# Gate vectors by weighted row sums inside the feed-forward networks, and one PSUM tile for both score maps of a differential head

## The chip, the cores and the metric

The program runs on one core of one Trainium2 chip. The metric is the device time of one execution in microseconds (us). The median of three runs of the kernel before is 1020.04 us (1017.32 to 1021.83).

## The reference, cut to what matters

One inference step of a two-layer backbone over 384 tokens, in three blocks of 128 (block 0 holds context tokens, blocks 1 and 2 latent ones), model width 1024. Each layer is a mixer, its output projection, and a SwiGLU network of width 2816. Layer 0 mixes by retention and windowed attention, layer 1 by differential attention and a Fourier transform. Each layer needs six modulation vectors per condition (there are two conditions: context and latent), one product of 1 x 1024 by 1024 x 6144:

```
mod = silu(cond) @ w_mod[l] + b_mod[l]
sh1, sc1, g1, sh2, sc2, g2 = split(mod, 6)
u = layer_norm(x) * (1 + sc1) + sh1
x = layer_norm(ALPHA * x + g1 * mixer(u), ...)
u = layer_norm(x) * (1 + sc2) + sh2
x = layer_norm(ALPHA * x + g2 * swiglu(u), ...)
```

The vector that the change is about is g2, number 5 of each layer's six, which is needed only once the network's output is complete. The other part is the differential attention, which has two score maps per head, each of 64 channels:

```
s = einsum('bqhmd,bkhmd->bhmqk', q, k) * 64 ** -0.5      # m = 0, 1
p = softmax(s);  p = p[:, :, 0] - lam * p[:, :, 1]
```

## The kernel before, in words

Everything lies in one program; when it is built, a planner fixes the order of instructions on each engine: of those that its own cost estimates show ready, the one of highest priority comes first (the order of the program text, raised by `boost`, L116). On the chip nothing overtakes on its engine. Matrix products with weights are split: a weight tile arrives by DMA (issued by SyncE's queue, SP) into a ring of five raw tiles, ScalarE casts it to a rounded copy (L173), VectorE makes the remainder (L175), and TensorE multiplies three times (rounded by rounded, and the two cross terms, L377, L518, L542). The copies lie in rings of five.

**The modulation vectors** are made in two ways. `mod_pe` (L223) loads a vector's 1024 x 1024 weights in eight raw tiles and multiplies each on TensorE with the conditions as a stationary operand of 32 columns: 32 matmuls of 128x256, four to a k-step. They are plain float32 matmuls, which stand as two records each in the trace, so 64 records for one vector. `mod_steps` (L237) loads the same eight tiles into another ring (`big`, four tiles, shared with the residual sums), and ScalarE (L246, first tile) and VectorE (L249, the seven others, two instructions each, one per condition) add them up with the conditions as per-partition weights into two tiles z; then eight matmuls with ones (16 records, L254) sum over the partitions, and two VectorE instructions (L258 or L260, L261) pick the rows. A gate vector (number 2 or 5) is then written to DRAM in eight small DMAs on SP (`mod_scratch`, L281) and read back broadcast by `load_g` (L414, two DMAs). Its bias comes by four DMAs on ScalarE's queue (L220).

**Where they run.** `WMODS` names the vectors that `w_out_phase` (L434) makes by `mod_pe`: g2 of layer 0 in layer 0's output projection, g2 of layer 1 in layer 1's. The order there is written by hand (`WORDER`, L38): P is the projection of a block with its residual, A and B its two layer norms, F the transposition to `u`, H the head of the network (its first 256 columns, gate `hg` and up `hu`, then the transposes `ht`), M the vector by `mod_pe`. M stands between the heads of blocks 1 and 2 (at the end: `X H1 M H2`). M's matmuls are not boosted and come late in the text, so the planner puts them where it has nothing else ready for TensorE. `SMODS` names the vectors that the network makes by `mod_steps`: five in layer 0, none in layer 1. The network (`ffn_phase`, L494) has ten rounds of two slots, each slot one projection (48 matmuls, L542) and, in the first 15 slots, one step of the down projection (18 matmuls, L518). A vector takes three slots: four weight tiles in each of the first two (`MSTEP`), a pause in the third; its last matmuls come at the next slot (`steps`, L1433). Five vectors take slots 0 to 14 of 20, and the last one's matmuls fall behind slot 15. The five last slots have no down step and are shorter.

**The differential scores** (`mixer_cd`, L1150). `scores` (L1245) works through 18 items (six heads, three blocks), two ahead. For an item, `sc1` (L1206) takes for each map one of four single-bank PSUM tiles, multiplies 64 channels (map 0 from partitions 0 to 63, map 1 from 64 to 127; 128 keys for block 0, else 384), and reduces the maximum over the keys (L1217); then one small instruction (L1219) and two exponentials (L1223). `sc2` (L1228) normalises, subtracts the maps (L1232 to L1234) and transposes (`td`). The items are mixed with the projections `cd` (L377) and the Fourier products (`y`, `z`). The window attention of layer 0 does its pair already as `sc1` does after the change: `win1` (L855) takes a pair of banks (`ws`) and one maximum for both (L872).

Of the kernel before, what the change touches and what calls it, by code (L numbers as in the profile page):

```python
# [14 lines left out]
AF = mybir.ActivationFunctionType  # L15
ALU = mybir.AluOpType
AX = mybir.AxisListType
PSUM = bass.MemoryType.PSUM

P = 128  # L20
# [5 lines left out]
NFP = D_FF // 256  # L26
HOLD = 4
RHOLD = (3, 5)
WMODS = (((0, 5),), ((1, 5),))
TMODS = ()  # L30
SMODS = (((1, 1), (1, 0), (1, 3), (1, 4), (1, 2)), ())
NLNW = 8
AORDER = "Q0 R0 W4 T G0 D V0 M0 Q1 W12 M1 G1 C0 E M2 N1 R1 N2 V1 C1 X N0 N4 N3 N5"
NIDLE = (5, 4)
# [30 lines left out]
def trunk_kernel(ctx: ExitStack, tc: tile.TileContext, a: dict):  # L65
    nc = tc.nc
    mm = nc.tensor.matmul
    V, S, G, SY = nc.vector, nc.scalar, nc.gpsimd, nc.sync
# [4 lines left out]
    def opened(name, **kw):  # L73
        st = ExitStack()
        return st.enter_context(pool(name, **kw)), st
# [6 lines left out]
    def bankA(name):  # L82
        return psA.tile([P, 512], F32, tag="A", name=name)
# [19 lines left out]
    def small(shape, name):  # L103
        tick[0] += 1
        n = 1
        for s in shape[1:]:
            n *= s
        return perm.tile(shape, F32, tag=f"sm{n}", name=f"{name}{tick[0]}", bufs=SMALL[n])
# [4 lines left out]
    def mid(shape, name):  # L113
        return perm.tile(shape, F32, tag="uf", name=name, bufs=3)

    def boost(f, *args, **kw):  # L116
        with tc.high_priority(offset=BOOST):
            return f(*args, **kw)  # L118

    def hmm(*args, **kw):  # L120
        return boost(mm, *args, **kw)
# [1028 lines left out]
    def mixer_cd(u, cat, pto, u1, t1):  # L1150
        o_k = a["o_diff_k"][0, 0].rearrange("t h m d -> t (h m d)")
        o_v = a["o_diff_v"][0, 0].rearrange("t h d -> t (h d)")
        slab = cd_slab
        bk = Banks("pcd", S=4)
        ap, ap_es = opened("attn_cd")
        rope_of[0] = ap.tile([P, 2, 2, 64], F32, name="rope1")
        S.dma_start(rope_of[0], a["k_rope"].rearrange("b p s d -> p b s d"))
        if True:
            nlam, sub = lamd["nlam"], lamd["sub"]
            dqT = ap.tile([P, H_DIFF, NTOK], F32, name="dqT")  # L1160
            dkT = ap.tile([P, H_DIFF, 512], F32, name="dkT")
# [4 lines left out]
            for i, n in ((0, 4), (4, 2)):  # L1166
                t = mid([P, 512], f"ck{i}")
# [38 lines left out]
            def sc1(b, h):  # L1206
                nk = 1 if b == 0 else 3
                k0 = 0 if b == 0 else P
                w = nk * P
                nm = small([P, 2], "dnm")  # L1210
                sums = small([P, 2], "dsum")
                pss = []
                for m in range(2):
                    rows = slice(64 * m, 64 * m + 64)
                    ps = bk("S", f"ds{b}_{h}_{m}")
                    hmm(ps[:, 0:w], dqT[rows, h, b * P : (b + 1) * P], dkT[rows, h, k0 : k0 + w], start=True, stop=True)
                    V.reduce_max(nm[:, m : m + 1], ps[:, 0:w], AX.X)  # L1217
                    pss.append(ps)
                V.tensor_scalar(nm, nm, -0.125, None, ALU.mult)  # L1219
                pm = []  # L1220
                for m in range(2):
                    t = ap.tile([P, 384], F32, tag="p", name=f"dp{b}_{h}_{m}", bufs=5)
                    S.activation(t[:, 0:w], pss[m][:, 0:w], AF.Exp, bias=nm[:, m : m + 1], scale=0.125,  # L1223
                                 accum_out=sums[:, m : m + 1])
                    pm.append(t)
                st_of[b, h] = (pm, sums)
# [18 lines left out]
            def scores(upto):  # L1245
                while state["n2"] < upto:
                    while state["n1"] < min(state["n2"] + 2, len(items)) and (state["n1"] < upto or upto == len(items)):
                        sc1(*items[state["n1"]])
                        state["n1"] += 1
                    sc2(*items[state["n2"]])  # L1250
                    state["n2"] += 1
# [59 lines left out]
            for b in range(NB):  # L1311
                ps = bankA(f"cd4_{b}")
# [6 lines left out]
            for b in range(NB):  # L1319
                ps = bankA(f"cd3_{b}")  # L1320
# [23 lines left out]
    m = {}  # L1344
    xscr = dram.tile([NB, P, D], F32, tag="xscr", name="xscr")
    for l in range(2):
# [9 lines left out]
        if l == 0:  # L1356
            def mod_ab(v, bk):
                mp = mod_pe(0, v, bk("M", f"mod0_{v}"))
                if v == 2:
                    m[0, v] = mod_scratch(mp, f"0_{v}")  # L1360
                else:
                    m[0, v] = mod_cols(mp, 0, v, bk("M", f"modt0_{v}"))

            pre, wxr_es = mixer_ab(u, cat, early, early_es, ap1, ap1_es, pto, *first, [lambda bk, v=v: mod_ab(v, bk) for v in (2, 3, 4)])
        else:
            cat, cat_es = open_cat(1)
            mixer_cd(u, cat, pto, m["s1"], m["t1"])
            pre, wxr_es = [], None
# [11 lines left out]
        hh = tuple(lnp.tile([P, NHEAD, NTOK], F32R, name=f"hh{q}{l}") for q in "rl")  # L1380
        w_out_phase(l, pre, cat, x, gt, lnv, u2, m[l, 3], m[l, 4], wx, hh, bankTO, WMODS[l])
        if wxr_es is not None:
# [37 lines left out]
        def all_mods(todo):  # L1420
            for ll, v in todo:
                out = []
                for pause in mod_steps(ll, v, out):
                    yield pause
                nm = f"{ll}_{v}"
                if v in (2, 5):
                    m[ll, v] = mod_scratch(out[0][0], nm)
                else:
                    m[ll, v] = mod_cols(out[0][0], ll, v, out[0][1])

        gen = all_mods(SMODS[l])

# [90 lines left out]
```

## Time and profile before

| | |
|---|---|
| median of three runs | 1020.04 us |
| profiled execution, its own time | 1018.55 us |
| its span in the trace | 1016.8 us |
| TensorE matmul busy, share of the span | 98% |
| VectorE busy | 63% |
| ScalarE busy | 43% |
| mean granted TensorE clock | 0.997 |

The span runs from the first to the last instruction of the profiled execution; 1.75 us of its own time lie outside. A line of the timeline is: start, duration, engine, line of the kernel, operation, output and inputs by the program's names, shapes, number of instructions merged, and in brackets the idle time before it and what ended that. The step from one row's start to the next row's start is the time that a stream of matmuls really takes; a row's own duration is longer, since matmuls overlap.

### The profile page before, as it was taken

To read this page: it belongs to the slowest core of one execution; us is meant where nothing else is said; L and a number is where in the kernel's file an instruction comes from. 1 tells how busy PE (TensorE), PEld (TensorE's weight loads), DVE (VectorE), ACT (ScalarE), POOL (GpSimd) and SP (SyncE) were. 2 spreads that over 40 slices of the span, in tenths; PEclk is the share of its full clock that TensorE was granted. 3 is DMA by queue.
4 is the path that set the end of the run, shared out by engine and by line. 5 is a ranking of instruction groups with operands and counts; after the bars stand their busy time and mean duration, and the time that the engine had idled before them with its cause. 6 is when DMAs were issued, how large, how long until landed. Compare 5 with 4: busy or idle time off the path is not lost.

```text
span 1016.8 us, 14891 instructions
## 1 busy us (share of the span) xinstructions
PE 996.9 (98%) x5679; PEld 829.7 (82%) x5679; DVE 637.9 (63%) x1356; ACT 432.9 (43%) x786; POOL 1.2 (0%) x5
## 2 busy tenths in 40 slices
PE   9999999999999999999999999999999999999996
PEld 4775567688898988989987766787889999999985
DVE  5477558588785977968567677558843333335554
ACT  3385533227543333333428555544833333333410
POOL 0000000000000000000000000000000000000000
PEclk9999999999999999999999999999999999999998
DMA  9975446472896767676615322235574444444401
GB/s 305 294 203 187 146 132 205 171 254 94 281 301 219 217 211 253 208 235 208 207 63 161 95 88 93 83 103 224 184 252 146 125 125 124 125 125 127 161 22 41
DMA packets 109703, 172.85 MB, mean 170 GB/s; under 512 B 10176, under 2 KB 78272, under 8 KB 109632
## 3 DMA queue, kind: packets, MB, share of 16 engines
q1 hardware_dynamic: 106960, 170.87, 52.8%
q10 hardware_dynamic: 2672, 1.04, 0.4%
q8 instruction: 44, 0.72, 0.3%
q14 instruction: 27, 0.22, 0.1%
HBM read 167.52 MB, written 4.36 MB: 169 GB/s over the span
## 4 chain that ended last, share of the span: by engine, by line
PE 91%; DMA 3%; DVE 3%; ACT 2%; issue 1%; ACTq 0%; DVEq 0%
PE dn L518 17%; PE wu L542 17%; PE wg L542 17%; PE cd L377 8%; PE wo L377 6%; PE rvg L377 3%; PE s L377 3%; PE rqk L377 2%; DMA rawm<-in_w_mod 2%; PE ds L118 2%; PE hg L377 2%; PE mod L118 1%; PE hu L377 1%; PE ms L118 1%; PE po L118 1%; PE wpo L118 1%
## 5 line engine op out<-in xcount | busy, mean ns | idle before, releaser
L542 PE MATMUL wg<-ulf,r_wg 128*128 128x384 f32 x320 | 108.4, 339 | 0.0
L542 PE MATMUL wu<-ulf,r_wu 128*128 128x384 f32 x320 | 108.3, 338 | 0.0
L542 PE MATMUL wu<-urf,r_wu 128*128 128x384 f32 x320 | 108.2, 339 | 0.0
L542 PE MATMUL wg<-urf,l_wg 128*128 128x384 f32 x320 | 108.1, 338 | 0.0
L542 PE MATMUL wu<-urf,l_wu 128*128 128x384 f32 x320 | 108.1, 338 | 0.0
L542 PE MATMUL wg<-urf,r_wg 128*128 128x384 f32 x320 | 108.0, 339 | 0.0
L175 DVE TENSOR_TENSOR l_wg<-raw_wg,r_wg 128x1024 fp32r<-128x1024 f32 x40 | 48.7, 1223 | 68.4 <-ACT r_wg L173 68.4
L249 DVE SCALAR_TENSOR_TENSOR z<-mraw,cs,z 128x1024 f32<-128x1024 f32 x70 | 86.3, 1280 | 8.3 <-DMA mraw<-in_w_mod 8.0
L175 DVE TENSOR_TENSOR l_wd<-raw_wd,r_wd 128x1024 fp32r<-128x1024 f32 x36 | 44.0, 1223 | 53.7 <-ACT r_wd L173 53.7
L173 ACT CAST r_wd<-raw_wd 128x1024 fp32r<-128x1024 f32 x36 | 37.8, 1050 | 87.0 <-PE wu L542 40.1
L175 DVE TENSOR_TENSOR l_wu<-raw_wu,r_wu 128x1024 fp32r<-128x1024 f32 x40 | 48.6, 1222 | 40.1 <-ACT r_wu L173 40.1
L173 ACT CAST r_wg<-raw_wg 128x1024 fp32r<-128x1024 f32 x40 | 42.0, 1050 | 73.0 <-PE dn L518 29.9
L173 ACT CAST r_wu<-raw_wu 128x1024 fp32r<-128x1024 f32 x40 | 42.0, 1049 | 64.6 <-issue 24.2
L518 PE MATMUL dn<-l_wd,hr 128*128 128x512 f32 x168 | 66.6, 396 | 0.0
L518 PE MATMUL dn<-r_wd,hr 128*128 128x512 f32 x168 | 66.5, 396 | 0.0
L518 PE MATMUL dn<-r_wd,hl 128*128 128x512 f32 x168 | 66.5, 396 | 0.0
L542 PEld LDWEIGHTS wg<-urf,r_wg 128*128 128x128 f32 x320 | 60.1, 188 | 1.9 <-issue 0.8
L542 PEld LDWEIGHTS wu<-urf,r_wu 128*128 128x128 f32 x320 | 60.1, 188 | 1.7 <-ACT r_wg L173 0.8
L542 PEld LDWEIGHTS wu<-ulf,r_wu 128*128 128x128 f32 x320 | 60.1, 188 | 0.5
L542 PEld LDWEIGHTS wg<-ulf,r_wg 128*128 128x128 f32 x320 | 60.1, 188 | 0.5
L542 PEld LDWEIGHTS wg<-urf,l_wg 128*128 128x128 f32 x320 | 60.1, 188 | 0.0
L542 PEld LDWEIGHTS wu<-urf,l_wu 128*128 128x128 f32 x320 | 60.1, 188 | 0.0
(418 smaller groups left out, 2180.0 us busy)
## 6 DMA issues: line engine op xcount, KB each, us to landing
raw_wd<-in_w_down SPq DMA_DIRECT2D x44, 512.0 KB
rawm<-in_w_mod SPq DMA_DIRECT2D x40, 512.0 KB
mraw<-in_w_mod SPq DMA_DIRECT2D x40, 512.0 KB
raw_wg<-in_w_gate SPq DMA_DIRECT2D x40, 512.0 KB
raw_wu<-in_w_up SPq DMA_DIRECT2D x40, 512.0 KB
raw_cd<-in_w_in_cd SPq DMA_DIRECT2D x20, 512.0 KB
ms<-in_w_mod SPq DMA_DIRECT2D x16, 512.0 KB
raw_rqk<-in_w_in_ab SPq DMA_DIRECT2D x16, 256.0 KB
```

The costliest lines, as they stand in the source:

```text
L118: return f(*args, **kw)
L173: S.copy(r, t)
L175: V.tensor_tensor(lo, t, r, ALU.subtract)
L249: V.scalar_tensor_tensor(z[c], t, cs[:, c, k : k + 1], z[c], ALU.mult, ALU.add)
L377: op = mm(ps[:, col : col + width], u[pu][:, k0 + kk, b * P : (b + 1) * P], (r, lo)[pw][:, kk, :], start=(first and i == 0 and pu + pw == ...
L518: mm(acc[b, nh], h[fc][ph][:, b * P : (b + 1) * P], wrl[pw][:, nh * 512 : (nh + 1) * 512], start=(fc == 0 and ph + pw == 0), stop=(last an ...
L542: mm(ps[j][:, 0:NTOK], un[i][pw][:, k, j * P : (j + 1) * P], u2[pu][:, 4 * i + k, :], start=(i == 0 and k == 0 and pu + pw == 0), stop=(i ...
```

## The change

Layer 0's g2 becomes the first of six vectors made by `mod_steps` in layer 0's network, layer 1's g2 the only one in layer 1's network; no vector is made in `w_out_phase` any more. In the differential scores the two maps of an item share a tile of two banks (two such tiles instead of four single ones), one instruction takes both maxima, and the exponentials read the halves.

```diff
-WMODS = (((0, 5),), ((1, 5),))
+WMODS = ((), ())
-SMODS = (((1, 1), (1, 0), (1, 3), (1, 4), (1, 2)), ())
+SMODS = (((0, 5), (1, 1), (1, 0), (1, 3), (1, 4), (1, 2)), ((1, 5),))
...
-        bk = Banks("pcd", S=4)
+        bk = Banks("pcd", S=2)
...
-                pss = []
+                ps = bk.pair("S", f"ds{b}_{h}")
                 for m in range(2):
                     rows = slice(64 * m, 64 * m + 64)
-                    ps = bk("S", f"ds{b}_{h}_{m}")
-                    hmm(ps[:, 0:w], dqT[rows, h, b * P : (b + 1) * P], dkT[rows, h, k0 : k0 + w], start=True, stop=True)
-                    V.reduce_max(nm[:, m : m + 1], ps[:, 0:w], AX.X)
-                    pss.append(ps)
+                    hmm(ps[:, m, 0:w], dqT[rows, h, b * P : (b + 1) * P], dkT[rows, h, k0 : k0 + w], start=True, stop=True)
+                V.reduce_max(nm, ps[:, :, 0:w], AX.X)
...
-                    S.activation(t[:, 0:w], pss[m][:, 0:w], AF.Exp, bias=nm[:, m : m + 1], scale=0.125,
+                    S.activation(t[:, 0:w], ps[:, m, 0:w], AF.Exp, bias=nm[:, m : m + 1], scale=0.125,
```

## Rows read from the trace of the kernel before

**Rows 1.** The page: the span, the busy time of three engines with its share and the number of instructions, and the chain that ended last by engine.
```profile
span 1016.8 us, 14891 instructions
PE 996.9 (98%) x5679; PEld 829.7 (82%) x5679; DVE 637.9 (63%) x1356; ACT 432.9 (43%) x786; POOL 1.2 (0%) x5
...
PE 91%; DMA 3%; DVE 3%; ACT 2%; issue 1%; ACTq 0%; DVEq 0%
```
**Rows 2.** Busy time by stretch: the end of layer 0's output phase, layer 0's network to the end of slot 15, its four last slots, the stretch of the scores, what follows them, and the end of layer 1's output phase. Columns: stretch and its length, busy us (instructions) of TensorE matmul, TensorE weight load, VectorE, ScalarE and GpSimd, granted clock, DMA share, GB/s.
```profile
245.40:270.80 25.40, 25.40 (x229) 21.38 (x229) 18.76 (x48) 19.68 (x36) 0.00 (x0) 1.00 0.62 205
270.80:476.20 205.40, 205.40 (x1122) 188.94 (x1120) 161.29 (x166) 72.98 (x89) 0.00 (x0) 1.00 0.74 236
476.20:511.10 34.90, 34.90 (x209) 34.28 (x209) 19.66 (x22) 15.91 (x20) 0.00 (x0) 1.00 0.62 195
574.40:640.30 65.90, 64.86 (x293) 42.55 (x292) 48.91 (x125) 36.40 (x100) 0.00 (x0) 1.00 0.23 72
640.30:673.50 33.20, 33.20 (x154) 26.34 (x152) 13.24 (x21) 16.03 (x36) 0.00 (x0) 1.00 0.26 91
719.70:744.80 25.10, 25.10 (x231) 21.47 (x230) 16.66 (x47) 16.85 (x34) 0.00 (x0) 1.00 0.62 201
```
**Rows 3.** The same view, of the instructions on the tile `mw` alone (the matmuls of `mod_pe` in the two output phases). Columns: stretch and length, busy us (records) of TensorE matmul, weight load and VectorE, granted clock, DMA share, GB/s.
```profile
245.40:270.80 25.40, 5.51 (x64) 1.93 (x64) 0.42 (x1) 1.00 0.62 205
719.70:744.80 25.10, 4.90 (x64) 1.79 (x64) 0.41 (x1) 1.00 0.62 201
```
**Rows 4.** The timeline at the end of layer 0's output phase (`hg`, `hu` head of the network, `urf`, `ulf` its input by the two halves of the channels).
```profile
252.40 1.07 PE L229 MATMUL mw<-rawm,cmod 128*32 128x256 f32 x16
253.77 1.50 PE L229 MATMUL mw<-rawm,cmod 128*32 128x256 f32 x22
254.14 0.62 ACT L332 CAST urf<-ufo 128x512 fp32r<-128x512 f32 x1
255.61 0.37 PE L377 MATMUL hg<-r_gh,urf 128*128 128x256 f32 x1
257.27 1.16 ACT L246 ACTIVATE z<-mraw,cs 128x1024 f32<-128x1024 f32 x1
261.49 0.69 DVE L333 TENSOR_TENSOR ulf<-ufo,urf 128x512 fp32r<-128x512 f32 x1
263.11 1.07 PE L229 MATMUL mw<-rawm,cmod 128*32 128x256 f32 x16
265.04 0.39 PE L377 MATMUL hg<-r_gh,urf 128*128 128x256 f32 x1
```
**Rows 5.** The same place in layer 1.
```profile
728.17 1.50 PE L229 MATMUL mw<-rawm,cmod 128*32 128x256 f32 x24
728.77 0.61 ACT L332 CAST urf<-ufo 128x512 fp32r<-128x512 f32 x1
729.60 0.39 PE L377 MATMUL hg<-r_gh,urf 128*128 128x256 f32 x1
736.33 0.69 DVE L333 TENSOR_TENSOR ulf<-ufo,urf 128x512 fp32r<-128x512 f32 x1
736.58 1.07 PE L229 MATMUL mw<-rawm,cmod 128*32 128x256 f32 x16
738.95 0.39 PE L377 MATMUL hg<-r_gh,urf 128*128 128x256 f32 x1
746.84 0.44 PE L118 MATMUL ht<-ident,hsg 128*128 128x128 f32 x2 [1.22 <-DVE hsg L480]
```
**Rows 6.** The vectors by row sums in layer 0's network: the group of all weighted sums on VectorE (busy us, mean ns of one, idle time before them), and the timeline of the last of the five vectors: the matmuls of the vector before it, its first and last sums, and its own matmuls.
```profile
L249 DVE SCALAR_TENSOR_TENSOR z<-mraw,cs,z 128x1024 f32<-128x1024 f32 x70 | 86.3, 1280 | 8.3 <-DMA mraw<-in_w_mod 8.0
...
440.79 1.07 PE L254 MATMUL mod<-z,ones 128*32 128x256 f32 x16
446.07 4.87 DVE L249 SCALAR_TENSOR_TENSOR z<-mraw,cs,z 128x1024 f32<-128x1024 f32 x4 [1.10 <-DMA mraw<-in_w_mod]
466.00 2.48 DVE L249 SCALAR_TENSOR_TENSOR z<-mraw,cs,z 128x1024 f32<-128x1024 f32 x2 [0.69 <-DMA mraw<-in_w_mod]
476.22 1.07 PE L254 MATMUL mod<-z,ones 128*32 128x256 f32 x16
```
**Rows 7.** The differential scores on TensorE: the tile `ds` in the stretch of the scores (columns as in Rows 2, without GpSimd), and the timeline of five places. An item's two matmuls are four records; the shapes are those of 128 keys and 384 keys.
```profile
574.40:640.30 65.90, 19.75 (x72) 8.10 (x72) 15.29 (x35) 17.95 (x65) 1.00 0.23 72
...
574.49 0.49 PE L118 MATMUL ds<-dkT,dqT 64*128 64x128 f32 x4
582.65 0.92 PE L118 MATMUL ds<-dkT,dqT 64*128 64x384 f32 x4
597.71 0.91 PE L118 MATMUL ds<-dkT,dqT 64*128 64x384 f32 x2
620.77 0.49 PE L118 MATMUL ds<-dkT,dqT 64*128 64x128 f32 x2 [0.70 <-ACT dp L1223]
```
**Rows 8.** Maxima on VectorE, by shape: of one score map (L1217), and of a pair in the window attention (L872). Busy us, mean ns of one, idle time before them.
```profile
L1217 DVE TENSOR_REDUCE dnm<-ds 128x1 f32<-128x384 f32 x24 | 12.9, 553 | 6.9 <-PE ds L118 6.6
L872 DVE TENSOR_REDUCE wnm<-ws 128x2 f32<-128x768 f32 x8 | 7.6, 956 | 4.0 <-PE ws L118 4.0
L1217 DVE TENSOR_REDUCE dnm<-ds 128x1 f32<-128x128 f32 x12 | 3.3, 285 | 5.4 <-PE ds L118 5.3
L872 DVE TENSOR_REDUCE wnm<-ws 128x2 f32<-128x256 f32 x4 | 1.7, 419 | 1.8 <-PE ws L118 1.7
```

## The prediction, made before the change was run

> **What bounds the kernel now.** I read the page first: TensorE is busy for 996.9 of 1016.8 us and holds 91% of the chain that ended last; VectorE is at 63%, ScalarE at 43% [rows 1]. Then the stretches that the change touches: in both output phases and in layer 0's network TensorE shows no free time at all, in the scores 1.0 us of 65.9, and the granted clock is 1.00 everywhere [rows 2]. So a matmul taken away counts only if the next one was ready behind it, and work added to VectorE counts only where VectorE then runs late. The second view is therefore the timeline around each removed piece: what would TensorE have waited for if the piece had not been there? The third is VectorE's free time per stretch. A matmul-busy figure is modelled, so I take what a piece occupies from the step between two starts wherever rows allow it.
>
> **1. The gate vector leaves the two output phases.** Removed per layer: 64 records on TensorE, 5.5 us in layer 0 and 4.9 us in layer 1 [rows 3], one addition on VectorE (0.4 us), eight weight loads on SP and eight small stores. These matmuls are filler, so much of them hides something.
> Layer 0. Two runs fill 252.40 to about 255.2, with two transposes between them. The head of block 1 needs `urf`, which is ready at 254.14 + 0.62 = 254.76, and it starts at 255.61 [rows 4]. With the filler gone TensorE stands idle for some 2 us instead; at best 0.8 us come back, and since a transposition of block 1 must still go first (its row is the puo step, about 0.4 us by the same kind of work), I take 0.4. The run at 263.11 and a short one behind it end at 265.04, where the head of block 2 starts. That needs only `ulf` of the first half, ready at 261.49 + 0.69 = 262.18 [rows 4]. Here nothing is hidden: 265.04 - 263.11 = 1.93, less some 0.4 for the transposes `ht` that stay (0.44 where they stand in layer 1 [rows 5]). Sum: -0.4 - 1.5 = -1.9, and -0.1 for a short run at a wait for `ulf`: **-2.0** (bounds -5.5, all of it, and 0: the idle time also pushes the chain of block 2's norms).
> Layer 1. The run at 728.17 covers the wait for `urf` (728.77 + 0.61 = 729.38; the head starts at 729.60): 0.2 come back. The runs from 736.58 to 738.95 stand where `ulf` is ready at 737.02 at the latest for the second pass, and the rounded pass can start before: 2.37 less 0.4 for `ht` [rows 5]. **-2.0** (bounds -4.9 and 0).
> Behind that, layer 1's network begins with a 1.22 us wait for `hsg` on VectorE [rows 5], where splits of the network's first weights, loaded late behind the vector's eight, stand ahead of it. With these loads gone from SP's queue the weights come earlier; layer 0 has no such wait. I take **-0.9** (bounds -1.2 and 0).
> Against it: ScalarE's first multiplications of the new vector come early, as layer 0's do, where one of 1.16 us stands between two pieces of a block's input [rows 4]. Layer 1 did not have them. **+0.5** (bounds 0 and 2 x 1.16).
>
> **2. The same vectors in the networks.** Added per layer: 16 records on TensorE, 1.07 us [rows 6]. TensorE is full there, so this is paid: **+2.1** (bounds 1.8 and 2.4). On VectorE 14 sums of 1.28 us and two additions, 19 us; on ScalarE two multiplications. Eight loads on SP replace eight; the four bias loads on ScalarE's queue and the eight stores move along, and so does the reading back (two DMAs), needed only behind the network's last matmul, some 200 us later in both layers: nothing.
> In layer 1 the vector takes the first slots, as the first of five does in layer 0 without an idle TensorE there [rows 2]: nothing. In layer 0 all five others move by three slots, so the sixth lies in the last ones. VectorE works 161.3 of 205.4 us up to there, and the shift changes little; but in 476.2 to 511.1 it now has 19.7 us to do in 34.9 [rows 2] and gets 17.9 + 1.0 more, 38.6 in all. What overflows are remainders made well ahead (of the held down-weights, of the next layer's first weights), so I take **+0.5** (bounds 0 and 3.7, the overflow; for more see the rivals).
>
> **3. The shared score tile.** On VectorE a pair's maximum takes 956 ns instead of 2 x 553, and 419 instead of 2 x 285 [rows 8]: 12 x 0.15 + 6 x 0.15 = 2.7 us less in a stretch where VectorE works 48.9 of 65.9 us [rows 2]: by itself nothing. The chain of an item gets longer by some 0.4 us, since a maximum starts after both maps; the projections fill that on TensorE, and they go on to 673 [rows 2].
> What counts is on TensorE. Both maps issued together (four records) take 0.92 us, one alone (two records) 0.91; for 128 keys 0.49 and 0.49 [rows 7]. Two matmuls of 64 channels from different halves of the partitions run side by side, if nothing stands between them. With single tiles the second map often waits until another exponential has freed its bank, and other work gets between; one such wait stands as 0.70 us idle [rows 7]. If all 18 items went as pairs, the scores would take 12 x 0.92 + 6 x 0.49 = 14.0 us; they take 19.75 [rows 7]. So 5.8 us are lost to parting, and each parted run costs a change between kinds of matmul too. A pair tile comes free as a whole, so both are ready together. A boosted transposition can still fall between; I reckon (an estimate) that a fifth stays parted: **-4.5** (bounds -7, with the changes of kind, and +1, if the longer chain stops TensorE once or twice as in that row).
>
> **A rule of the Trainium skill that speaks against it.** In the stretch of the scores the weight loads fill 42.55 of 65.9 us, 65%, against 98% for the matmuls [rows 2]. The Trainium skill ("Perfetto Trace Analysis", section "Identifying the Most-Contended Engine") calls matmul busy time a poor measure of how near TensorE is to its limit, and wants the share of weight loads beside it. By that the stretch has a third of its time in hand and part 3 would be worth nothing: the sum would be -1.8 instead of -6.3. I hold to the step between starts, which shows records of a lone map taking a pair's time.
>
> **The sum.** -2.0 - 2.0 - 0.9 + 0.5 + 2.1 + 0.5 - 4.5 = -6.3. The profiled execution took 1018.55, so 1012.25; the median of the runs shown is 1.49 higher, which gives **1013.7 us**, 0.6% below the median.
>
> **The rivals.**
> *The scores are not limited by TensorE.* The time won there turns into waiting for the maxima and exponentials, whose chain is longer now. For it: the 0.70 us wait, and VectorE at 74% of that stretch. Against: only 1.0 us idle in 65.9, and projections that fill. The sum without part 3: 1013.7 + 4.5 = 1018.2. Chance 0.15. The rule of the Trainium skill above would have it so.
> *Pairs stay parted.* The shared tile does not do what counts, because transposes and projections stand between its two matmuls in the planned order. For it: the order is planned, not chosen on the chip. Then part 3 gives about -0.5: 1017.7. Chance 0.12.
> *The cover is worth all of it.* The idle time in the output phases takes the whole removal back, the matmuls in the networks are paid: 1013.7 + 4.0 = 1017.7. For it: the filler stands exactly where inputs come late [rows 4, 5]. Chance 0.08.
> *The sixth vector stops TensorE (slower).* Place: layer 0's network behind its last round. The vector's matmuls belong behind slot 18, three of the four slots that fill 477.3 to 511.1 (8.45 us each), so at about 502.7. Its sums can start only when the vector before has freed its tiles: 446.07 - 440.79 = 5.3 us behind 476.22, at 481.5 [rows 6]. 17.9 us of sums and the share of VectorE's other work in that time (19.7 of 34.9, so 12.0 in 21.2 us [rows 2]) end at about 511.4. If the planner leaves the matmuls at 502.7 on TensorE, everything behind them waits 8.7 us; the overflow of 3.7 then also meets the residual at the end. 1013.7 + 8.7 = 1022.4, up to 1026.1. It decides if the matmuls are placed before about 511. Against: before, the sums ended at 468.5, some 8 us ahead of their matmuls at 476.22, and the planner sees the same load [rows 6]. Chance 0.10.
>
> **How the numbers follow.** Forecast 0.55, rivals 0.15, 0.12, 0.08, 0.10. About 0.5% (5.1 us) is what a measurement of this kernel can tell from no change. The forecast's own range is 1007 to 1017: part 3 at -7 and part 1 with half of its cover on the one side, the chosen costs at their upper bounds on the other. Faster by over 0.5% is below 1014.9: most of the forecast's case, 0.48, and 0.04 of the others where the rest comes out better: 0.52. Slower by over 0.5% is above 1025.1: the upper part of the last rival and nothing else, with something for a mishap in the new order: 0.08. The rest, 0.40, is the same. The range to hold it 8 times in 10 runs from 1006.5, beyond which lies 0.08, to 1020.0, which takes in the three rivals on the same side.
>
> **What would show it.** Part 1: in the output phases idle TensorE of about 2 us where the first filler stood, and the head of block 2 starting some 2 us after its input's first half no longer. Part 2: 16 records `mod` per network, and behind slot 18 no wait on z. Part 3: `ds` busy near 15 us, rows of four records, and no `ds` wait over 1 us. I am wrong if `ds` falls and the projections behind it end no earlier, if TensorE waits for z near 503 to 511, or if the heads of block 2 start as late as before.

## The result and the profile after

The median went from 1019.37 us (six runs, 1017.32 to 1021.83) to **1012.97 us** (six runs, 1012.03 to 1014.77). The ratio is 0.994 with a 95% interval of 0.9923 to 0.9957, so 4.4 to 7.8 us were won; 1013.7 had been forecast. Run again beside later experiments, the changed kernel had 1013.19 us against 1019.1, ratio 0.9942 (0.9930 to 0.9954). The profiled execution took 1012.87 us.

The page of the changed kernel, beside [rows 1]:
```profile
span 1011.1 us, 14717 instructions
...
PE 984.2 (97%) x5583; PEld 824.0 (81%) x5583; DVE 668.2 (66%) x1368; ACT 436.5 (43%) x790; POOL 1.2 (0%) x5
```
TensorE has 96 records fewer (2 x 64 removed, 2 x 16 added) and 12.7 us less of busy time; VectorE has 30.3 us more. The stretches of [rows 2] in the changed kernel, columns as there (end of layer 0's output phase, its network up to slot 16, the network's last slots, the scores and what follows, the end of layer 1's output phase):
```profile
243.40:266.60 23.20, 20.47 (x164) 19.57 (x165) 19.34 (x49) 19.54 (x36) 0.00 (x0) 1.00 0.46 141
266.60:474.40 207.80, 206.06 (x1134) 188.92 (x1132) 159.91 (x164) 73.89 (x90) 0.00 (x0) 1.00 0.71 225
474.40:514.30 39.90, 38.56 (x227) 36.58 (x224) 35.82 (x39) 15.96 (x21) 0.00 (x0) 1.00 0.73 236
575.20:640.00 64.80, 62.55 (x309) 42.61 (x308) 49.89 (x113) 39.05 (x110) 0.00 (x0) 1.00 0.24 74
640.00:669.10 29.10, 29.06 (x134) 23.32 (x135) 10.78 (x14) 13.24 (x27) 0.00 (x0) 1.00 0.31 104
715.50:739.20 23.70, 20.72 (x165) 19.66 (x165) 18.89 (x49) 19.49 (x36) 0.00 (x0) 1.00 0.47 149
```
See two things. Both output phases are shorter though TensorE now stands idle in them (2.73 and 2.98 us): the filler is gone and part of what it covered shows. And layer 0's network, which had no idle TensorE, has 1.74 us of it up to slot 16 and 1.34 us behind.

The time from one landmark on TensorE to the next shows where it went. Each is the start of a first matmul in the timeline; the columns run from the first `wo` to the first `wg` (output phase 0), from there to the first `cd` (network 0), from the first `ds` to the first `dpv` (scores), from the head `hg` of layer 1 to its slot 2 (output phase 1), and from there to slot 18 (network 1). One profiled execution each, us:
```
                                 output 0  network 0  scores  output 1  network 1
before                              66.36     270.60   92.85     51.93     181.63
changed kernel                      64.10     275.50   87.79     49.31     182.85
the same again (e9)                 65.37     272.58   87.81     49.33     183.04
shared tile alone (e1)              66.37     271.42   87.78     51.39     181.56
gate vectors alone (e2)             64.10     272.78   92.87     49.32     182.99
layer 1's vector and tile (e3)      66.35     270.62   87.78     49.32     182.68
the same again (e12)                66.37     271.33   87.78     49.32     183.01
layer 0's vector and tile (e6)      65.51     277.52   87.83     50.58     182.01
two maxima (e4)                     65.34     275.37   88.21     49.31     183.16
before, one item ahead (e5)         66.37     271.34   90.44     51.47     181.75
sums spread (e7)                    64.12     273.60   87.77     49.31     182.93
same half of the partitions (e8)    65.31     276.04   93.46     49.33     183.23
sums end early (e10)                65.38     274.89   87.77     49.48     183.25
load one ahead (e11)                64.02     273.70   87.76     49.35     182.88
```
With the same code the scores repeat within 0.1 us, output phase 1 without its vector within 0.2 (with it, 50.6 to 51.9), network 1 within 0.6. Network 0 does not repeat, and output phase 0 has two values, which is the second half of this story. From before to after: -2.26, +4.90, -5.06, -2.62, +1.22, and -1.97 ahead of the first `wo`. There TensorE's order is unchanged; over the fourteen executions that landmark lies between 202.51 and 205.31, so the -1.97 is chance and no gain. A profiled execution is also not always a typical one: that of e6 took 1019.39 us, the most of its twelve, beside a median of 1014.14, and that of e2 1016.94, the least of its twelve, beside 1018.91.

**Where the scores won.** The whole stretch in the kernel before, and its `ds` matmuls:
```profile
574.49:667.34 92.85, 91.81 (x412) 63.87 (x412) 58.36 (x140) 48.36 (x125) 0.00 (x0) 1.00 0.24 78
...
574.49:667.34 92.85, 19.75 (x72) 8.10 (x72) 16.11 (x36) 20.18 (x72) 1.00 0.24 78
```
and in the changed kernel, and behind them three rows of its timeline:
```profile
575.18:662.97 87.79, 85.51 (x412) 60.94 (x411) 56.91 (x122) 48.34 (x125) 0.00 (x0) 1.00 0.26 83
...
575.18:662.97 87.79, 13.67 (x72) 5.51 (x72) 13.94 (x18) 20.04 (x72) 1.00 0.26 83
```
```profile
583.33 0.92 PE L118 MATMUL ds<-dkT,dqT 64*128 64x384 f32 x4
584.18 0.50 PE L377 MATMUL cd<-l_cd,ur 128*128 128x512 f32 x1
625.34 0.30 PE L118 MATMUL td<-ident,dp 128*128 128x128 f32 x1 [0.50 <-DVE dnm L1217]
```
The same 72 records take 6.08 us less, and the stretch is 5.06 us shorter. The difference is TensorE's idle time, 1.04 before and 2.28 after: the maximum of a pair starts when both maps are there, and the transposes `td` wait up to 0.50 us for it.

**What layer 0's network gave back.** Round 3 of the changed kernel, VectorE, then TensorE:
```profile
338.33 2.48 DVE L249 SCALAR_TENSOR_TENSOR z<-mraw,cs,z 128x1024 f32<-128x1024 f32 x2 [2.95 <-DMA mraw<-in_w_mod]
340.73 0.55 DVE L559 TENSOR_TENSOR sg<-wu,sg 128x384 f32<-128x384 f32 x1
341.20 1.22 DVE L175 TENSOR_TENSOR l_wd<-raw_wd,r_wd 128x1024 fp32r<-128x1024 f32 x1
342.33 4.87 DVE L249 SCALAR_TENSOR_TENSOR z<-mraw,cs,z 128x1024 f32<-128x1024 f32 x4
347.12 0.55 DVE L566 TENSOR_TENSOR hl<-sg,hr 128x384 fp32r<-128x384 f32 x1
347.58 0.55 DVE L559 TENSOR_TENSOR sg<-wu,sg 128x384 f32<-128x384 f32 x1
...
346.11 0.34 PE L542 MATMUL wg<-urf,r_wg 128*128 128x384 f32 x1
348.19 0.44 PE L542 MATMUL wg<-urf,r_wg 128*128 128x384 f32 x1 [1.74 <-DVE sg L559]
```
A weighted sum waits 2.95 us for its weights by DMA, four more stand behind it, and `sg`, the product that frees TensorE's PSUM tile, is queued behind all of them. The same kernel run again (e9), the same place:
```profile
338.58 2.48 DVE L249 SCALAR_TENSOR_TENSOR z<-mraw,cs,z 128x1024 f32<-128x1024 f32 x2 [0.58 <-DMA mraw<-in_w_mod]
340.98 0.55 DVE L559 TENSOR_TENSOR sg<-wu,sg 128x384 f32<-128x384 f32 x1
...
345.50 2.48 DVE L249 SCALAR_TENSOR_TENSOR z<-mraw,cs,z 128x1024 f32<-128x1024 f32 x2 [0.44 <-DMA mraw<-in_w_mod]
347.89 0.55 DVE L566 TENSOR_TENSOR hl<-sg,hr 128x384 fp32r<-128x384 f32 x1
348.36 0.55 DVE L559 TENSOR_TENSOR sg<-wu,sg 128x384 f32<-128x384 f32 x1
```
Here the weights came 2.4 us sooner, and no wait of TensorE over 0.2 us is left in the network. The other executions with the same order of instructions in this network go the same way: where the weights came 2.95 to 3.25 us late (the changed kernel, e4, e6, e8) TensorE waited 1.74 to 2.09 us, and where VectorE stood idle for them 0.58 us or less (e9, e2) it did not wait there. The last slots of the changed kernel, TensorE, then VectorE:
```profile
480.01 0.41 PE L542 MATMUL wg<-urf,r_wg 128*128 128x384 f32 x1 [0.61 <-DVE modc L272]
500.38 0.44 PE L542 MATMUL wg<-urf,r_wg 128*128 128x384 f32 x1 [0.73 <-ACT sg L552]
504.78 1.07 PE L254 MATMUL mod<-z,ones 128*32 128x256 f32 x16
...
494.20 5.07 DVE L249 SCALAR_TENSOR_TENSOR z<-mraw,cs,z 128x1024 f32<-128x1024 f32 x4 [0.51 <-DMA mraw<-in_w_mod]
499.66 0.55 DVE L559 TENSOR_TENSOR sg<-wu,sg 128x384 f32<-128x384 f32 x1
501.26 2.48 DVE L249 SCALAR_TENSOR_TENSOR z<-mraw,cs,z 128x1024 f32<-128x1024 f32 x2
```
The sixth vector's sums end at 503.7, before its matmuls at 504.78: the long wait of the slower rival is not there, but two short ones are.

Round 3 is the part that changes from execution to execution; the steady loss lies behind it. From slot 16 to the first `cd` the six executions with this order took 66.51 to 67.96 us, mean 67.34, and the five without the sixth vector 64.11 to 64.23, mean 64.18: 3.16 us more. The eight new matmuls are 1.00 of them, four small records that used to come before slot 16 are 0.36, and idle TensorE is some 0.8; the rest, some 1 us, is in slightly longer steps around these places and was not taken apart. Up to slot 16 the same means differ by 0.74 us.

### The profile page after: what moved, and what is told of

It reads as the page before. It is cut to its first block, busy times and chain, and to the rows that moved or that the text cites. A ratio compares the mean times of both kernels' runs of the same rounds, so it can differ in the third digit from the quotient of the medians.

```text
span 1011.1 us, 14717 instructions
## 1 busy us (share of the span) xinstructions
PE 984.2 (97%) x5583; PEld 824.0 (81%) x5583; DVE 668.2 (66%) x1368; ACT 436.5 (43%) x790; POOL 1.2 (0%) x5
## 3 DMA queue, kind: packets, MB, share of 16 engines
q10 hardware_dynamic: 2672, 1.04, 0.4%
## 4 chain that ended last, share of the span: by engine, by line
PE 81%; DVE 8%; DMA 4%; ACT 4%; issue 2%; ACTq 0%; DVEq 0%
PE dn L518 17%; PE wg L542 15%; PE wu L542 15%; PE cd L377 7%; PE wo L377 4%; PE rvg L377 3%; PE s L377 3%; DMA rawm<-in_w_mod 2%; PE rqk L377 2%; PE mod L118 2%; DVE z L249 1%; PE ms L118 1%; PE hg L377 1%; PE wpo L118 1%; PE idle L129 1%
## 5 line engine op out<-in xcount | busy, mean ns | idle before, releaser
L249 DVE SCALAR_TENSOR_TENSOR z<-mraw,cs,z 128x1024 f32<-128x1024 f32 x98 | 121.0, 1281 | 12.0 <-DMA mraw<-in_w_mod 11.5
```

Source lines behind the costliest of these rows:

```text
L249: V.scalar_tensor_tensor(z[c], t, cs[:, c, k : k + 1], z[c], ALU.mult, ALU.add)
```

## The experiments

The kernels ran in three groups (e1, e2, e3, e6; then e4, e5, e7, e8; then e9 to e12), each group on one chip beside the kernel before. Medians, and ratios to the kernel before with their 95% intervals.

**e1: the shared tile alone.**
```
 WMODS = (((0, 5),), ((1, 5),))
 SMODS = (((1, 1), (1, 0), (1, 3), (1, 4), (1, 2)), ())
```
Expected: 

> Only the shared score tile; both gate vectors stay in the output phases. Theory A (the steps of the two traces: -2.2 us in layer 0's output phase, +4.9 in layer 0's network, -5.0 in the scores, -2.7 in layer 1's output phase and the start of its network, +1.2 in that network; some 2 us ahead of all that are chance): about 5.0 us below the kernel before, 0.995 of it, ds busy 14 to 15.5 us in place of 19.75, nothing else moved. Rival B (what TensorE wins in the scores is given back behind them, and the gate vectors bring the whole): within 2 us of the kernel before, though ds falls.


Measured: 1015.05 us against 1018.9, ratio 0.9955 (0.9941 to 0.9969). The scores take 87.78 us, as in the changed kernel. This part is worth 3.2 to 6.0 us by itself, the trace's 5.07 among them.

**e2: the gate vectors alone.** The score tiles of the kernel before, WMODS and SMODS of the change.
Expected: 

> Only the two gate vectors moved into the networks; single score tiles. Theory A: -2.2 + 4.9 - 2.7 + 1.2 = +1.2 us, the same as the kernel before (1.000 to 1.002). Rival B: -4 to -6 us, 0.995.


Measured: 1018.91 against 1018.9, ratio 1.0003 (0.9991 to 1.0016). Nothing is won. The trace shows gains and losses that nearly cancel: output phases -2.26 and -2.61, networks +2.18 and +1.36.

**e3 and e6: one vector each, with the shared tile.** e3 leaves layer 0's vector in its output phase:
```
-WMODS = ((), ())
+WMODS = (((0, 5),), ())
-SMODS = (((0, 5), (1, 1), (1, 0), (1, 3), (1, 4), (1, 2)), ((1, 5),))
+SMODS = (((1, 1), (1, 0), (1, 3), (1, 4), (1, 2)), ((1, 5),))
```
e6 does it the other way round, with layer 1's vector left in place.
Expected of e3: 

> The shared score tile, and layer 1's gate vector in its network; layer 0's stays in its output phase. Theory A: -5.0 - 2.7 + 1.2 = -6.5 us against the kernel before and 2.7 us below the changed kernel, since layer 0's network keeps five vectors and no idle TensorE. Rival C (the waits in layer 0's network came from somewhere else, or the sixth vector costs no more than its matmuls): 1 to 2 us above the changed kernel, since the 2.2 us of layer 0's output phase are lost.


Expected of e6: 

> The shared score tile, and layer 0's gate vector in its network; layer 1's stays in its output phase. Theory A: -2.2 + 4.9 - 5.0 = -2.3 us against the kernel before, so 4 us worse than e3; TensorE idle for some 3 us in layer 0's network. Rival C: -2.2 + 1.1 - 5.0 = -6 us, as good as e3 or better.


Measured: e3 1013.84, ratio 0.9952 (0.9936 to 0.9969); e6 1014.14, ratio 0.9962 (0.9946 to 0.9978). The medians, 0.3 us apart, do not part them, and bear out neither the 4 us of theory A nor rival C. The traces differ: without the sixth vector layer 0's network takes 270.62 us (e3), with it 277.52 (e6, in the slowest of its twelve executions). In e6 the wait of round 3 was 2.09 us long, and something came behind it. The windows around it (columns as in [rows 2]):
```profile
350.00:352.00 2.00, 0.47 (x3) 0.14 (x1) 2.00 (x4) 0.00 (x0) 0.00 (x0) 1.00 1.07 350
352.00:354.00 2.00, 1.44 (x4) 1.44 (x5) 2.00 (x4) 0.52 (x1) 0.00 (x0) 0.63 0.85 295
354.00:356.00 2.00, 2.00 (x8) 2.00 (x8) 1.25 (x2) 1.02 (x1) 0.00 (x0) 0.52 1.02 371
356.00:358.00 2.00, 2.00 (x13) 2.00 (x12) 0.57 (x1) 1.17 (x2) 0.00 (x0) 1.00 0.72 218
```
The granted clock is 0.52 in the second stretch behind the wait, the lower of TensorE's two levels (1.2 GHz), with 8 matmuls where the next two microseconds have 13. From slot 6 to slot 8 this execution lost 3.87 us, of which the wait is 2.09. Behind the 1.74 us wait of the changed kernel the clock stayed at 1.00, as it did behind those of 2.03 us in e4 and 1.95 us in e8.

**e4: two maxima on the shared tile.** Is it the single maximum that counts?
```
-                V.reduce_max(nm, ps[:, :, 0:w], AX.X)
+                for m in range(2):
+                    V.reduce_max(nm[:, m : m + 1], ps[:, m, 0:w], AX.X)
```
Expected: 

> The changed kernel, but the maximum of a shared score tile is taken in two instructions, one for each map. Theory (what counts in the shared tile is that its two score matmuls are issued together): the scores on TensorE stay at 13 to 14.5 us busy, VectorE does some 2.7 us more beside them, time within 1 us of the changed kernel (1012.0 to 1014.0). Rival (the single maximum counts, VectorE limits the stretch): the gain of the stretch is lost, 1015.5 to 1018.


Measured: 1014.7 against 1019.1, ratio 0.9950 (0.9931 to 0.9969); `ds` 14.30 us busy, the scores 88.21 us. The time is 0.7 us above the range, but the stretch itself lost only 0.42 us. The single maximum counts for next to nothing; what is issued together counts.

**e5: single tiles, one item ahead.** The kernel before, with
```
-                    while state["n1"] < min(state["n2"] + 2, len(items)) and ...
+                    while state["n1"] < min(state["n2"] + 1, len(items)) and ...
```
Expected: 

> The kernel before with its single score tiles, but only one item of scores issued ahead instead of two, so that a second map seldom waits for a bank. Theory (parting came from waits for banks): the scores fall from 19.75 us busy to 13 to 16, and the dpv matmuls start 3 to 5 us earlier, if the shorter lead does not stop TensorE at the exponentials (that would show as idle time before the transposes td, up to 0.5 us for each of 18 items). Time 1014.5 to 1018. Rival (parting comes from the planned order itself, or the second tile frees late anyway): scores stay at 18 to 20 us, time 1018 to 1025.


Measured: 1015.88, ratio 0.9969 (0.9955 to 0.9982); `ds` 17.12 us busy, above the 13 to 16 expected, the scores 90.44 us. With less ahead fewer pairs are parted, and the kernel is faster by 3.2 us without any shared tile. The scores gain 2.41 us, less than the 3 to 5 expected: more than half of the parted time stays, and three times TensorE still waits for an exponential to free a bank (1.3 us in all). That supports the cause named in the prediction, the wait for banks, for part of the parting.

**e8: both maps from the same half.** Map 1's scores are those of map 0 here; that part of the result is left out.
```
-                    rows = slice(64 * m, 64 * m + 64)
+                    rows = slice(0, 64)
```
Expected: 

> The changed kernel, but both maps of a shared score tile are taken from partitions 0 to 63, so that map 1's scores are those of map 0 (that part of the result is left out). Theory (the two matmuls run beside each other because they lie in different halves of the partitions): one behind the other they take twice the time, the scores rise from 13.7 to 25 to 27 us busy, and the time by 10 to 12.6 us, to 1022 to 1026. Rival (adjacency alone counts, whatever the partitions; or the stretch is not limited by TensorE): scores at 13 to 15 us, or the time stays within 2 us of the changed kernel.


Measured: 1019.06, ratio 0.9994 (0.9978 to 1.0011): the whole gain is gone. A pair in the timeline, and the stretch with its `ds`:
```profile
587.70 1.55 PE L118 MATMUL ds<-dkT,dqT 64*128 64x384 f32 x4
589.18 0.50 PE L377 MATMUL cd<-l_cd,ur 128*128 128x512 f32 x1
```
```profile
579.32:672.78 93.46, 93.46 (x412) 66.71 (x411) 57.51 (x122) 48.63 (x125) 0.00 (x0) 1.00 0.24 78
...
579.32:672.78 93.46, 22.64 (x72) 11.20 (x72) 14.01 (x18) 20.06 (x72) 1.00 0.24 78
```
From start to start a pair takes 1.48 us instead of 0.85. The theory's kind was right, its size was not: 1.48 is less than twice 0.85, so 22.64 and not 25 to 27 us, and the stretch grows by 5.67 us, not by 10 to 12.6, in part because 2.28 us of idle TensorE are used up first. By this the two matmuls run beside each other because they lie in different halves of the partitions. The Trainium skill ("TensorE: Matmul & The Clock Gate", section "Part 3: Packing small matmuls — row/col tiling") says that matmuls in different row groups of the array run concurrently; the trace agrees, 0.85 against 1.48 us.

**e7: the sums spread.**
```
-MSTEP = 4
+MSTEP = 3
...
-                    st["pause"] = 1
```
Expected: 

> The changed kernel, but the work of the gate vectors inside the networks is handed out in steps of three instead of four and without a pause behind a vector. Theory (the 2 to 5 us that layer 0's network gives back are waits for VectorE where sums stand in clumps ahead of a silu product): the waits of wg and wu there shrink from 3 us to under 1 us, layer 0's network ends 1 to 3 us earlier, time 1010 to 1012.5. Rival (the loss is TensorE's own work and chance of arrival): same time, 1012.5 to 1014. Second rival (slower hand-out moves the sixth vector's sums to the end of the network, and the residual waits for them): 1015 to 1020.


Measured: 1013.66 against 1019.1, ratio 0.9944 (0.9926 to 0.9961), as the changed kernel and in the rival's range. In its profile the wait of round 3 is gone (205.84 us up to slot 16, against 207.85), although the weights came late here too, on VectorE:
```profile
340.55 2.48 DVE L249 SCALAR_TENSOR_TENSOR z<-mraw,cs,z 128x1024 f32<-128x1024 f32 x2 [2.37 <-DMA mraw<-in_w_mod]
```
With fewer sums behind the late one, `sg` came in time. This is one execution, and e9 has no wait there without the edit, so for the rounds the theory is supported and not proven. For the end it missed: the last slots still take 67.76 us (64.22 before).

**e9: the changed kernel again.**
Expected: 

> The changed kernel once more, as the measure for the other three of this group. Expected by both theories: 1012 to 1014.5, ratio to the kernel before 0.993 to 0.996. Theory (the wait in round 3 of layer 0's network is a weighted sum that waits for its weights by DMA): that wait lies between 0 and 2.1 us from execution to execution, and in the profile it is as long as the idle time of VectorE at mraw just before allows.


Measured: 1013.19, as given above. The profile shows no wait in round 3, whose two slots take 27.19 us (26.99 before, 29.00 in the first execution), behind an idle time of 0.58 us at `mraw` where the first execution had 2.95.

**e10: the sums end early.**
```
-MSTEP = 4
+MSTEP = 3
...
             for _ in range(MSTEP):
-                if next(gen, False):
-                    st["pause"] = 1
-                    return
+                next(gen, False)
```
Expected: 

> The changed kernel, but the weight tiles of the six vectors are handed out three to a slot without a pause and without a break between vectors, so 48 tiles fill slots 0 to 15 and the last five short slots hold no sums. Theory (the end of layer 0's network lost 2 us because 17.9 us of sums fell into the stretch where VectorE has 15 us to spare): the stretch from slot 16 to the start of cd goes back from 67.65 to 65 to 66 us (the eight matmuls stay), the waits at its modc and sg go; rounds 3 to 7 may lose up to 1 us. Time 1010.5 to 1012.5. Rival (VectorE is then too full in the slots before, 180 of 205 us): waits of wg and wu of 2 to 5 us there, 1013 to 1017.


Measured: 1014.4 against 1019.1, ratio 0.9958 (0.9946 to 0.9970). The theory missed, and the time lies in the rival's range: the last slots take 67.47 us, hardly less than the 67.65 of the changed kernel. The sums end at 480.6, but a new wait has come. TensorE, then VectorE:
```profile
490.34 0.42 PE L542 MATMUL wu<-urf,r_wu 128*128 128x384 f32 x1 [1.44 <-DVE bm L261]
...
488.57 1.23 DVE L175 TENSOR_TENSOR hwl<-raw_wd,hwr 128x1024 fp32r<-128x1024 f32 x1 [1.71 <-ACT hwr L173]
489.72 0.48 DVE L261 SCALAR_TENSOR_TENSOR bm<-mod,selc,bm 128x256 f32<-128x256 f32 x1
```
The two small instructions that empty the vector's PSUM tile (L258, L261) got a remainder between them that waits 1.71 us for ScalarE. So it is not the sums alone: whatever waits at the head of VectorE's queue holds up what TensorE needs.

**e11: each weight tile loaded one ahead.**
```
+        def fetch(k):
+            ts[k] = big([P, D], f"mraw{l}_{v}_{k}")
+            SY.dma_start(ts[k], w[:, k, v * D : (v + 1) * D])
...
+        fetch(0)
         for k in range(KC):
-            t = big([P, D], f"mraw{l}_{v}_{k}")
-            SY.dma_start(t, w[:, k, v * D : (v + 1) * D])
+            if k + 1 < KC:
+                fetch(k + 1)
+            t = ts.pop(k)
```
Expected: 

> The changed kernel, but inside a vector of the networks each weight tile's load is issued one tile earlier, ahead of the sums of the tile before. Theory (VectorE stands at a sum whose weights are late, and the silu products queue behind it): the wait of wg at sg in round 3 falls from 1.74 us to below 0.7 us, the network's rounds up to slot 16 take 206 to 206.5 us instead of 207.85, time 0.5 to 1.5 us below the changed kernel. Rival (the weights come at the pace of the DMA queues whatever the order of issue, or the earlier load delays the network's own weights): no difference, or 0.5 to 2 us longer.


Measured: 1012.35 against 1019.1, ratio 0.9935 (0.9923 to 0.9947), 0.8 below e9 and inside its interval. Up to slot 16 the network takes 205.83 us, but e9 had 206.06 without the edit, so this does not show that the load ahead did it.

**e12: e3 again, beside e9.**
Expected: 

> Layer 0's gate vector left in the output phase as before, layer 1's inside its network, shared score tile as in the change; beside the changed kernel on the same chip. Theory (layer 0's network gives back all that its output phase gained, and more): output phase 0 takes 2.15 us more than in the changed kernel, layer 0's network 3 to 5 us less; time 1 to 3 us below the changed kernel. Rival (only the sums' chance of arrival differs, the two places are worth the same): within 0.7 us of it.


Measured: 1012.5 against 1019.1, ratio 0.9931 (0.9918 to 0.9944); 0.7 below e9, intervals overlapping. The theory's sizes missed: output phase 0 takes 1.00 us more than in e9 and layer 0's network 1.25 less, and the time is what the rival allows. No kernel of the twelve is shown to beat the changed one.

**Why output phase 0 has two values.** Nine of the executions have layer 0's vector out of that phase: four take 64.0 to 64.1 us and five 65.3 to 65.5. The changed kernel is of the first kind, and waits there three times within ten microseconds:
```profile
244.83 0.38 PE L377 MATMUL hg<-r_gh,ulf 128*128 128x256 f32 x1 [0.98 <-DVE ulf L333]
...
251.61 0.44 PE L118 MATMUL ht<-ident,hsg 128*128 128x128 f32 x2 [0.57 <-DVE hsg L480]
253.22 0.66 PE L118 MATMUL puo<-ident,so 128*128 128x128 f32 x4 [1.18 <-DVE hhl L392]
```
e9 has the same three waits (0.98, 0.57 and 1.19 us) and is of the second kind. The windows behind the last wait, the changed kernel's first, then e9's:
```profile
252.00:254.60 2.60, 1.42 (x12) 1.33 (x12) 2.06 (x11) 1.86 (x6) 0.00 (x0) 1.00 0.99 315
254.60:257.20 2.60, 2.60 (x23) 2.50 (x23) 1.03 (x3) 2.60 (x6) 0.00 (x0) 1.00 0.06 22
```
```profile
253.30:256.00 2.70, 1.51 (x9) 1.43 (x9) 2.08 (x11) 1.82 (x6) 0.00 (x0) 0.81 0.96 322
256.00:258.60 2.60, 2.60 (x16) 2.60 (x15) 0.92 (x2) 2.46 (x5) 0.00 (x0) 0.55 0.04 14
```
In e9 the granted clock is 0.55 there, the lower level for most of the window, and 16 matmuls run where the other has 23. That is the 1.27 us between the two kinds. All five of the second kind show it (0.50 to 0.71 in a like window); all four of the first kind have 1.00, and so have the five executions that kept the filler. The idle time that the removed filler left thus costs more than itself in some executions; why the same kernel is found among both kinds is not shown. In layer 1's output phase, with waits of 0.93 and 1.32 us, the clock was 1.00 in every execution.

## Why the prediction was right, point by point

**The forecast held** (1013.7; 1012.97, and 1013.19 again), and with it part 3 as the main gain. By terms, from the profiled executions:

Part 1, layer 0: -2.0, measured -2.26 in the changed kernel and -0.99 in e9. The working named the place and the size; it did not know that the clock could take half of it back. Part 1, layer 1 with the wait for `hsg` and the +0.5 on ScalarE: together -2.4, measured -2.62. The 1.22 us wait [rows 5] is gone, but a new one appeared at the head of block 2, where `hsg` stands behind a table load on ScalarE that the filler had covered:
```profile
725.39 0.39 PE L377 MATMUL hg<-r_gh,urf 128*128 128x256 f32 x1 [1.32 <-ACT hsg L477]
...
723.66 1.28 ACT L477 ACT_TABLE_LOAD   x1
```
The +0.5 was meant for early multiplications on ScalarE. One of them, 1.14 us long, does stand ahead of this table load, which begins 8.15 us behind the first `hg` (7.42 before); how much of the wait of 1.32 us is its doing was not measured. The table load the prediction did not name.

Part 2: 1.07 per network for the matmuls, measured 1.00 in network 0's rows and +1.22 for the whole of network 1. **The term that failed is layer 0's network, +0.5 for VectorE's overflow.** Six executions with this code took 272.58 to 277.52 us, mean 274.97; five without the sixth vector took 270.60 to 271.42, mean 271.06. So in these profiles the vector cost 3.9 us in the mean and not 1.6; without e6, the slowest, the mean is 3.4, and in e9 and e2, with no wait in round 3, it is 1.5 and 1.7, about what was forecast. The step looked only at the balance of busy time per stretch, and only at the last slots. Up to slot 16 it was not a lack of time: VectorE did 159.91 us of work in 207.80, less than before. It was the order on VectorE, where a sum waits for its weights and `sg` stands behind it (1.74 us, in round 3, earlier than the step looked). In the last slots, where most of the mean cost lies, VectorE was busy for 35.82 of 39.90 us, and TensorE had small waits at `modc` and `sg` (0.61 and 0.73 us); there order and lack of time are not told apart, since ending the sums early (e10) only brought another wait.

Part 3: -4.5, measured -5.06 (e1: -5.07). No pair stayed parted: every row of `ds` holds four records, or eight, where an estimate had left a fifth apart. The longer chain did cost something, 1.2 us of idle TensorE.

The rivals. *Scores not limited by TensorE*: the rows refute it for this stretch. Weight loads filled 63.87 of 92.85 us, 69%, and yet 6.08 us less of matmuls made the stretch 5.06 us shorter, while e8's longer matmuls filled it to 93.46 of 93.46. The trace thus does not bear out the rule of the Trainium skill ("Perfetto Trace Analysis", section "Identifying the Most-Contended Engine") as the prediction used it, by the weight loads alone; the section names a second measure beside them, the matmuls' share of the peak rate of arithmetic, which is not worked out here. *Pairs stay parted*: refuted by the rows of `ds`. *The cover is worth all of it*: for the vectors together the times of e2 say so (ratio 1.0003), but by another way, since the output phases did win 4.9 us and the networks took 3.5. Beside the shared tile the vectors may bring a little (0.994 with both, 0.9955 in e1 without), but the intervals overlap. *The sixth vector stops TensorE*: right in place and kind, wrong in size: the planner put the sums ahead of the remainders, so they ended at 503.7 and not at 511.4, and the 8.7 us became 1.34.

The sum was closer than its terms, and that is in good part luck. In the profiled execution +3.3 too much in network 0 stood against -1.97 of chance ahead of the first `wo`, -0.26 in output phase 0, -0.22 in output phase 1 and -0.56 in the scores.

**What stays open.** The profiled executions put layer 0's half of the move at a loss: 3.9 us in the network against 1.6 us won in the output phase (66.36 to a mean of 64.8). The medians do not show a loss (e12 0.7 below e9, e6 0.9 below e1, each inside the intervals), so whether that half should be undone is not settled.

## What to carry to other kernels

Two small matmuls that can run beside each other are worth a pair only if nothing gets between them: give them one tile, so that they become ready together, and read the step between starts to see whether they did. Before work is moved to an engine with free time, ask what stands behind it in that engine's queue and what it waits for itself; a share of busy time shows neither. Filler on TensorE that covers waits is cheaper than its busy time says; here the clock also fell in layer 0's output phase in five of nine executions without the filler and in none of five with it.

## What the runs showed of the hardware that was not expected

Idle stretches of TensorE of 0.98, 0.57 and 1.19 us within ten microseconds, with matmuls between them, were followed by a granted clock at the lower level in five of nine executions, at a cost of some 1.3 us, and not in the other four; the same kernel is found among both. One wait of 2.09 us was followed by it too; waits of 2.03, 1.95 and 1.74 us at the same place in three other executions were not. And two score matmuls from the same half of the partitions took 1.48 us from start to start in e8, less than twice the 0.84 from the start of one alone to the next row's start in the kernel before.
